# The filter's normalisation, one channel tile per attention step

## The chip, the cores and the metric

The kernel runs on one core of one Trainium2 chip. The metric is device time in microseconds of one execution, the median of several runs. Engines by their short names: PE (TensorE, matmuls; PEld its weight loads), DVE (VectorE), ACT (ScalarE), POOL (GpSimd), SP (which issues the DMAs).

## The reference, cut to what matters

One decoder block over 512 tokens of 1024 channels: an attention branch (16 heads, three kinds of keys) and a convolution branch, merged by sigmoid gates, then a projection, a SwiGLU feed-forward and a last norm. The change touches the middle of the convolution branch, a layer norm over the channels of each token and a Silu:

```
z  = u_a * sigmoid(u_b)                         # 512 tokens x 1024 channels
z  = causal_depthwise_conv(z, 31 taps) + conv_b
mu = mean(z, channels);  var = mean((z - mu)**2, channels)
zn = (z - mu) * rsqrt(var + EPS) * ln_g + ln_b
conv = silu(zn) @ w_conv_out + b_conv_out
```

## The kernel before

Activations lie with channels on the partitions: eight tiles `ct` of 128 channels x 512 tokens hold the filter's output. A sum over the channels is a matmul with `ones` (each entry 1/1024), which leaves the same mean in every partition.

The attention is a loop of 32 units (`n`): four key groups, two pairs of heads in each, four blocks of 128 queries. A unit first scores (`sc`: matmuls, maximum on DVE, exponential on ACT), then transposes the probabilities (`tP`), splits them into a high and a low part (`pth` by ACT, `ptl` by DVE) and multiplies with the values (`pv`). The loop interleaves the scoring of one unit with the second half of the last. Each step of it calls one piece of attention, then one of `taps`, then `fill`, which puts dense projections (`pch`, `ptk`) of some 520 ns of PE time between. All dense matmuls run as three products of high and low parts, whose weights ACT casts (`wh`) and POOL or DVE subtracts (`wl`).

`conv_taps` yields after every tap of a channel tile: one `scalar_tensor_tensor` on DVE, which accumulates in a PSUM bank (tag `cv`, one buffer; the loop's four tiles use it one after the other). In the loop run the taps of tiles 4 to 7, 4 x 31 steps.

`conv_norm` is called behind units 16, 17, 18, 20 and 21 (`stages`), each time with a whole stage: POOL sums the eight tiles (0); PE takes the mean over the partitions, ACT copies it to SBUF and DVE subtracts it from eight tiles (1); ACT squares and POOL sums (2); PE takes the variance, ACT the root by Sqrt and DVE its reciprocal (3); DVE multiplies eight tiles and ACT takes eight Silus, with the norm's scale and bias per channel (4). The sums over partitions use banks of tag `tr`, of which there are two and which the transposes use too; the squares use tiles of tag `pt`, five buffers, as `pth` and `ptl` do. At unit 24 `y_split` splits the eight tiles for the output projection.

The program is written in one order. Each engine's queue is then laid down before the run by a planner, which estimates when inputs are ready and buffers are free, and on the chip each engine runs its queue in that order.

Of the kernel before, what the change touches and what calls it, by code (L numbers as in the profile page):

```python
# [10 lines left out]
F32 = mybir.dt.float32  # L11
# [3 lines left out]
AF = mybir.ActivationFunctionType  # L15
OP = mybir.AluOpType
# [4 lines left out]
S = 512  # L21
KT = D // 128
NT = S // 128
# [5 lines left out]
EPS = 1e-6  # L29
# [7 lines left out]
def hybrid_block(  # L37
# [8 lines left out]
    nc = tc.nc  # L46
# [4 lines left out]
    cp = ctx.enter_context(tc.tile_pool(name="const", bufs=1))  # L51
# [5 lines left out]
    ps = psum_a.enter_context(tc.tile_pool(name="ps", bufs=1, space=PSUM))  # L57
# [4 lines left out]
    pa = astack.enter_context(tc.tile_pool(name="att", bufs=1))  # L62

    def acts(name, dt=F32):
        return ap.tile([128, S], dt, name=name, tag="A")

    def mid(name, tag="Z"):
        return bp.tile([128, 544 if tag == "Z" else S], F32, name=name, tag=tag)
# [10 lines left out]
    def scp(name):  # L79
        return ps.tile([128, 512], F32, name=name, tag="sc", bufs=2)  # L80

    def trp(name):
        return ps.tile([128, 512], F32, name=name, tag="tr", bufs=2)


    idn = cp.tile([128, 128], F32, name="idn")
# [3 lines left out]
    ones = cp.tile([128, 128], F32, name="ones")  # L90
    nc.vector.memset(ones, 1.0 / D)
    half = cp.tile([128, 4], F32, name="half")
    nc.vector.memset(half, -0.5)
    epsc = cp.tile([128, 1], F32, name="epsc")
# [67 lines left out]
    nc.tensor.transpose(pv0[:, :48], vst, idn[:48, :48])  # L162
    vec = cp.tile([128, 6, 8], F32, name="vec")
    nc.vector.tensor_copy(vec.rearrange("p a b -> p (a b)"), pv0[:, :48])
    g_mix, cb, lng, lnb, bco, g_ffn = (vec[:, i, :] for i in range(6))

    hT_hi = [acts(f"hThi{k}", F32R) for k in range(KT)]
    hT_lo = [acts(f"hTlo{k}", F32R) for k in range(KT)]
# [15 lines left out]
    for th in range(2):  # L184
# [6 lines left out]
        for k in range(KT):  # L191
            p = trp("hT")
# [161 lines left out]
    def ub_g(c, **kw):  # L354
        def ev(m, p):
            z = zs[2 * c + m]
            nc.vector.memset(z[:, 0:TAPS - 1], 0.0)
            z_done[0] = nc.scalar.activation(z[:, TAPS - 1:TAPS - 1 + S], p, AF.Tanh, scale=0.5).ins

        return chan_g(w_in, C_UB + 256 * c, hT_hi, hT_lo, ev, **kw)  # L360

    def ua_g(c):
        def ev(m, p):
            z = zs[2 * c + m][:, TAPS - 1:TAPS - 1 + S]
            nc.vector.scalar_tensor_tensor(z, z, 1.0, p, op0=OP.add, op1=OP.mult)

        return chan_g(w_in, C_UA + 256 * c, hT_hi, hT_lo, ev)

    def run_all(*gens):
        gens = list(gens)  # L370
        while gens:
            for g_ in list(gens):
                if next(g_, gens) is gens:
                    gens.remove(g_)
# [407 lines left out]
    def conv_taps(chans):  # L782

        acc = {}
        for k, c in enumerate(chans):
            cts[c] = mid(f"ct{c}", "C")
            acc[c] = ps.tile([128, 512], F32, name="cacc", tag="cv", bufs=1) if k == 0 else scp("cacc")
        for j in range(TAPS):
            for c in chans:
                z, a = zs[c], acc[c]  # L790
                if j == 0:
                    nc.scalar.activation(a, z[:, 0:S], AF.Identity, scale=cw[:, 0, c:c + 1], bias=cb[:, c:c + 1])  # L792
                else:
                    nc.vector.scalar_tensor_tensor(cts[c] if j == TAPS - 1 else a, z[:, j:j + S], cw[:, j, c:c + 1],  # L794
                                                   a, op0=OP.mult, op1=OP.add)
                yield 0

    norm = {}
    stages = [16, 17, 18, 20, 21]

    def conv_norm(stage):
        cc = [c[:, :S] for c in cts]
        if stage == 0:
            acc = pa.tile([128, S], F32, name="acc", tag="acc", bufs=1)
            nc.gpsimd.tensor_add(acc, cc[0], cc[1])
            for c in range(2, 8):
                nc.gpsimd.tensor_add(acc, acc, cc[c])
            norm["sum"] = acc
        elif stage == 1:
            p = trp("pstat")  # L810
            nc.tensor.matmul(p, ones, norm["sum"], start=True, stop=True)
            mean = pa.tile([128, S], F32, name="mean", tag="acc", bufs=1)
            nc.scalar.copy(mean, p)
            for c in range(8):
                nc.vector.tensor_sub(cc[c], cc[c], mean)
        elif stage == 2:
            acc = pa.tile([128, S], F32, name="acc2", tag="acc", bufs=1)
            nc.scalar.activation(acc, cc[0], AF.Square)
            for c in range(1, 8):
                sq = pa.tile([128, S], F32, name="sq", tag="pt", bufs=5)  # L820
                nc.scalar.activation(sq, cc[c], AF.Square)
                nc.gpsimd.tensor_add(acc, acc, sq)
            norm["sum"] = acc
        elif stage == 3:
            p = trp("pvar")
            nc.tensor.matmul(p, ones, norm["sum"], start=True, stop=True)
            rs = pa.tile([128, S], F32, name="rs", tag="acc", bufs=1)
            nc.scalar.activation(rs, p, AF.Sqrt, bias=epsc)
            nc.vector.reciprocal(rs, rs)
            norm["rs"] = rs  # L830
        elif stage == 4:
            for c in range(8):
                nc.vector.tensor_mul(cc[c], cc[c], norm["rs"])
            for c in range(8):
                nc.scalar.activation(cc[c], cc[c], AF.Silu, scale=lng[:, c:c + 1], bias=lnb[:, c:c + 1])

    ma, gcs = [], []
    phase["early"] = False
# [15 lines left out]
    def ga_g(g):  # L854
        gts[g] = [mid("gt") for _ in range(2)]
        return tanh_tiles(C_GA + 256 * g, [t_[:, :S] for t_ in gts[g]])
# [3 lines left out]
    def y_split():  # L860
        for c in range(8):
            cc = cts[c][:, :S]
            hi, lo = acts(f"yh{c}", F32R), acts(f"yl{c}", F32R)
            nc.scalar.copy(hi, cc)
            nc.vector.tensor_sub(lo, cc, hi.bitcast(F32))
            y_hi.append(hi)
            y_lo.append(lo)
# [53 lines left out]
    fin_v(*hid_v)  # L921
    qs[0, 1] = query_split(qds[0], 1)
    run_all(conv_taps((2, 3)))
    taps = itertools.chain(*(conv_taps((c,)) for c in range(4, 8)))
    work = []
    debt = [0.0]

# [10 lines left out]
    def fill_until(gen):  # L938
        while gen in work:
            c = next(work[0], None)  # L940
            if c is None:
                work.pop(0)
            elif c:
                debt[0] -= c
# [9 lines left out]
    for n in range(32):  # L954
        g, pr, i = n // 8, n // 4 % 2, n % 4
        if n % 8 == 0:
            for g_ in need:
                fill_until(g_)
            if g < 3:
                qds[g + 1] = []  # L960
                need = [query_dense(g + 1, qds[g + 1]), ga_g(g + 1)]
                work += ([ub_g(3), ua_g(3)] if g == 0 else []) + need
            if g == 0:
                gx = bp.tile([128, 1024], F32, name="gx", tag="gx", bufs=1)
                work.append(gc_g([gx[:, 0:512], gx[:, 512:1024]]))
            else:
                work.append(gc_key())
            if g:
                qs[g, 0] = query_split(qds[g], 0)
        if i == 0:  # L970
            ma.append(gts[g][pr])
        cur = unit(g, qs[g, pr], i, ma[-1], pr)
        na, nc_ = (2, 4, 4, 6)[i], ((n - 1) % 4 + 3 if n else 0)
        f = 520 if n < 24 else 800
        for gen in mixed(cur, na, pend, nc_):
            next(gen, None)
            next(taps, None)
            fill(f)
        pend = cur
        if n == 24:  # L980
            fill_until(work[-1] if work else None)
            y_split()
            work += [conv_out_g(c) for c in range(4)]
        if n == 25:
            qs[3, 1] = query_split(qds[3], 1)
            for t in range(2):
                load_x1(t, rp, "qd")
        elif g and n % 8 == 1:
            qs[g, 1] = query_split(qds[g], 1)
        if n == 29:  # L990
            while work:
                fill_until(work[-1])
            for ch in range(7):
                merge(ch)
        if n == 30:
            merge(7, (0,))
            phase["lo_dve"] = True
            work += [w_out_g(0, c) for c in range(2)]
        if n in stages:
            for _ in taps:  # L1000
                pass
            conv_norm(stages.index(n))
    for _ in pend:
        fill(800)
    while work:
# [116 lines left out]
    for t in range(NT):  # L1122
        sl = slice(128 * t, 128 * t + 128)

        for c in ((0, 256), (256, 512)) if t == NT - 1 else ((0, 512),):
# [5 lines left out]
            if j == 1 and t == NT - 1:  # L1131
                nc.vector.tensor_scalar(s01[:, t:t + 1], sums[:, t, 1:2], 1.0 / D, s01[:, t:t + 1], op0=OP.mult,
                                        op1=OP.add)
        r = cp.tile([128, 1], F32, name="rstd", tag="rstd", bufs=4)
# [6 lines left out]
                                       op0=OP.mult, op1=OP.mult)  # L1141
# [28 lines left out]
```

## Time and profile before

| | us |
|---|---|
| median of three runs (lowest, highest) | 975.17 (974.79, 975.36) |
| the profiled execution | 974.84 |
| its span, first to last instruction | 973.1 |
| PE busy | 940.4 |
| DVE, ACT, POOL busy | 633.1, 545.1, 234.9 |

The profile is of one execution. Times in it count from the first instruction. The attention loop runs from about 215 to 575 us. Busy time of PE is an upper bound of its work, since matmuls are pipelined and overlap.

### The profile page before, as it was taken

Reading aid. Unit: us, or ns where it says so; the run is one execution under the profiler, and the core shown is the slowest. Engines: PE = TensorE matmul, PEld = TensorE weight load, DVE = VectorE, ACT = ScalarE, POOL = GpSimd, SP = SyncE. Lnnn points to the kernel's source line nnn. Section 1 sums busy time; section 2 is a strip of 40 time slices with the busy share of each in tenths; the row PEclk is TensorE's granted clock in tenths of the full one; section 3 lists DMA queues with packets and bytes.
Section 4 is the critical chain, followed back from the end, with each engine's and each line's share of the span. In section 5 each row is a group of like instructions: output and inputs, shape, how many; then the busy total and the mean of one; then the engine's idle time right before and its main releaser. Section 6 shows DMA issues by size and latency. Waiting matters only on the chain.

```text
span 973.1 us, 14959 instructions
## 1 busy us (share of the span) xinstructions
PE 940.4 (97%) x5306; PEld 797.5 (82%) x5306; DVE 633.1 (65%) x1254; ACT 545.1 (56%) x1273; POOL 234.9 (24%) x256
## 2 busy tenths in 40 slices
PE   5999989899999999989999999999999999999996
PEld 5889979888888977877778878988888888888886
DVE  6799999987999987676876877633333343322512
ACT  6533545558879887999984776533333333322412
POOL 3545447853353342622322000000000000000000
PEclk9999989999999999999999999999999999999999
DMA  7333324542121111111212166633333323322302
GB/s 225 90 106 88 87 72 121 134 109 55 45 66 44 34 45 44 44 33 55 98 56 76 59 201 188 180 96 100 91 105 88 107 87 108 97 96 95 118 29 87
DMA packets 77599, 89.03 MB, mean 91 GB/s; under 512 B 5896, under 2 KB 65620, under 8 KB 77524
## 3 DMA queue, kind: packets, MB, share of 16 engines
q1 hardware_dynamic: 76676, 87.38, 30.0%
q8 instruction: 42, 0.69, 0.3%
q0 software_dynamic: 144, 0.52, 0.2%
q14 instruction: 33, 0.27, 0.1%
q10 hardware_dynamic: 704, 0.17, 0.1%
HBM read 85.96 MB, written 2.10 MB: 90 GB/s over the span
## 4 chain that ended last, share of the span: by engine, by line
PE 85%; DVE 7%; ACT 4%; issue 1%; DMA 1%; POOL 1%; SPq 0%; POOLq 0%; ACTq 0%; DVEq 0%
PE pf L211 8%; PE pf L212 8%; PE pf L213 8%; PE pch L213 7%; PE pch L211 7%; PE pch L212 7%; PE ptk L211 4%; PE ptk L212 4%; PE ptk L213 4%; PE pd L211 4%; PE pd L213 4%; PE pd L212 4%; PE tP L732 3%; PE sc L700 2%; PE sc L701 2%; PE pv L756 2%
## 5 line engine op out<-in xcount | busy, mean ns | idle before, releaser
L137 POOL TENSOR_TENSOR wl<-wr,wh 128x512 fp32r<-128x512 f32 x128 | 167.2, 1318 | 229.8 <-ACT wh L136 179.5
L136 ACT CAST wh<-wr 128x512 fp32r<-128x512 f32 x228 | 140.1, 622 | 145.0 <-PE pf L212 52.6
L794 DVE SCALAR_TENSOR_TENSOR cacc<-z,cw,cacc 128x512 f32<-128x512 f32 x232 | 165.5, 748 | 3.8 <-ACT cacc L792 1.7
L211 PE MATMUL pf<-h2hi,wh 128*128 128x512 f32 (+1 forms) x384 | 142.3, 372 | 0.6 <-ACT h2hi L1034 0.6
L212 PE MATMUL pf<-h2lo,wh 128*128 128x512 f32 (+1 forms) x384 | 142.5, 372 | 0.0
L213 PE MATMUL pf<-h2hi,wl 128*128 128x512 f32 (+1 forms) x384 | 142.4, 372 | 0.0
L137 DVE TENSOR_TENSOR wl<-wr,wh 128x512 fp32r<-128x512 f32 x100 | 68.7, 689 | 109.6 <-ACT wh L136 108.1
L213 PE MATMUL pch<-hThi,wl 128*128 128x512 f32 (+1 forms) x272 | 107.3, 395 | 1.5 <-POOL wl L137 1.5
L211 PE MATMUL pch<-hThi,wh 128*128 128x512 f32 (+1 forms) x272 | 107.3, 396 | 1.2 <-ACT hThi L195 1.2
L212 PE MATMUL pch<-hTlo,wh 128*128 128x512 f32 (+1 forms) x272 | 107.5, 396 | 0.0
L149 DVE TENSOR_TENSOR wl<-wr,wh 128x512 fp32r<-128x512 f32 x76 | 51.6, 689 | 61.9 <-ACT wh L148 61.8
L148 ACT CAST wh<-wr 128x512 fp32r<-128x512 f32 (+1 forms) x84 | 50.1, 604 | 73.7 <-PE pd L213 50.9
L708 ACT ACTIVATE P<-sc,nm 128x32 f32<-128x32 f32 (+3 forms) x192 | 84.7, 446 | 11.2 <-DVE nm L705 9.2
L1136 POOL TENSOR_TENSOR rstd<-rstd,half 128x1 f32<-128x1 f32 x4 | 2.2, 547 | 359.6 <-DVE rstd L1135 359.6
L211 PEld LDWEIGHTS pf<-h2hi,wh 128*128 128x128 f32 x384 | 72.0, 188 | 13.2 <-ACT h2hi L1034 0.8
L211 PE MATMUL ptk<-wh,hThi 128*128 128x256 f32 x288 | 82.7, 287 | 0.0
L213 PEld LDWEIGHTS pf<-h2hi,wl 128*128 128x128 f32 x384 | 72.2, 188 | 12.6
L212 PEld LDWEIGHTS pf<-h2lo,wh 128*128 128x128 f32 x384 | 72.2, 188 | 12.4
L212 PE MATMUL ptk<-wl,hThi 128*128 128x256 f32 x288 | 81.2, 282 | 0.0
L213 PE MATMUL ptk<-wh,hTlo 128*128 128x256 f32 x288 | 81.0, 281 | 0.0
L705 DVE TENSOR_REDUCE nm<-sc 128x1 f32<-128x32 f32 (+3 forms) x192 | 68.8, 381 | 16.8 <-PE sc L703 15.5
L211 PE MATMUL pd<-wh,ahi 128*128 128x512 f32 (+1 forms) x184 | 70.0, 380 | 0.8 <-DVE x L1092 0.8
(234 smaller groups left out, 2133.0 us busy)
## 6 DMA issues: line engine op xcount, KB each, us to landing
wr<-in_w_in_dram SPq DMA_DIRECT2D x100, 256.0 KB, 2.8
wr<-in_w_ffn_gate_dram SPq DMA_DIRECT2D x48, 256.0 KB, 2.7
wr<-in_w_ffn_up_dram SPq DMA_DIRECT2D x48, 256.0 KB, 2.7
wr<-in_w_ffn_down_dram SPq DMA_DIRECT2D x44, 256.0 KB, 2.5
wr<-in_w_out_dram SPq DMA_DIRECT2D x32, 256.0 KB, 2.6
x<-in_x_dram SPq DMA_DIRECT2D x8, 512.0 KB, 5.0
wr<-in_w_conv_out_dram SPq DMA_DIRECT2D x16, 256.0 KB, 2.7
wr<-in_cmp_k_w_dram SPq DMA_DIRECT2D x8, 256.0 KB, 2.6
```

The source lines that it names most:

```text
L136: nc.scalar.copy(hi[:, sl, :ncol], raw[:, sl, :ncol])
L137: eng.tensor_sub(lo[:, sl, :ncol], raw[:, sl, :ncol], hi[:, sl, :ncol].bitcast(F32))
L148: nc.scalar.copy(hi, raw)
L149: (nc.vector if phase["lo_dve"] else nc.gpsimd).tensor_sub(lo, raw, hi.bitcast(F32))
L211: nc.tensor.matmul(o, lh, rh, start=first, stop=False, skip_group_check=True)
L212: nc.tensor.matmul(o, lh, rl, start=False, stop=False, skip_group_check=True)
L213: nc.tensor.matmul(o, ll, rh, start=False, stop=last, skip_group_check=True)
L700: nc.tensor.matmul(sc[:, :e - a], qh[:, tsl], K[:, a:e], start=True, stop=False)
L705: nc.vector.tensor_reduce(out=nm[:, b:b + 1], in_=sc[:, ba - a:be - a], axis=AX.X, op=OP.max, negate=True)
L708: nc.scalar.activation(P[:, ba:be], sc[:, ba - a:be - a], AF.Exp, bias=nm[:, b:b + 1], accum_out=Dn[:, b, hh:hh + 1])
L732: nc.tensor.transpose(t4[:, 256 * b + 128 * hh:256 * b + 128 * hh + 128], Ps[hh][:, key_blk(j, b)], idn)
L794: nc.vector.scalar_tensor_tensor(cts[c] if j == TAPS - 1 else a, z[:, j:j + S], cw[:, j, c:c + 1], a, op0=OP.mult, op1=OP.add)
```

## The change

Stages are gone: `conv_norm` is now a generator, chained behind the taps, so that each step of the attention loop takes one piece of it. The mean stays in the bank `cv` and DVE subtracts from there; after each subtraction the same step squares on ACT and adds on POOL. The variance is taken by four matmuls with the sum of squares as weights and one column of `ones`, which puts it on 128 tokens by four columns; DVE adds EPS, POOL raises to the power -0.5, and four matmuls of the result, broadcast, with the identity spread it over the partitions into bank `cv` again. The Silu becomes x/2 (1 + tanh(x/2)): ACT writes the tanh to the bank `cv` and the halved affine to the tile, and DVE joins them by one `scalar_tensor_tensor`. `lnh` holds the halved scale and bias.

```
--- before.py
+++ after.py
@@ -162,7 +162,9 @@
     nc.tensor.transpose(pv0[:, :48], vst, idn[:48, :48])
     vec = cp.tile([128, 6, 8], F32, name="vec")
     nc.vector.tensor_copy(vec.rearrange("p a b -> p (a b)"), pv0[:, :48])
-    g_mix, cb, lng, lnb, bco, g_ffn = (vec[:, i, :] for i in range(6))
+    g_mix, cb, _, _, bco, g_ffn = (vec[:, i, :] for i in range(6))
+    lnh = cp.tile([128, 2, 8], F32, name="lnh")
+    nc.vector.tensor_scalar(lnh, vec[:, 2:4, :], 0.5, None, op0=OP.mult)
 
     hT_hi = [acts(f"hThi{k}", F32R) for k in range(KT)]
     hT_lo = [acts(f"hTlo{k}", F32R) for k in range(KT)]
@@ -795,44 +797,45 @@
                                                    a, op0=OP.mult, op1=OP.add)
                 yield 0
 
-    norm = {}
-    stages = [16, 17, 18, 20, 21]
-
-    def conv_norm(stage):
+    def conv_norm():
+
         cc = [c[:, :S] for c in cts]
-        if stage == 0:
-            acc = pa.tile([128, S], F32, name="acc", tag="acc", bufs=1)
-            nc.gpsimd.tensor_add(acc, cc[0], cc[1])
-            for c in range(2, 8):
-                nc.gpsimd.tensor_add(acc, acc, cc[c])
-            norm["sum"] = acc
-        elif stage == 1:
-            p = trp("pstat")
-            nc.tensor.matmul(p, ones, norm["sum"], start=True, stop=True)
-            mean = pa.tile([128, S], F32, name="mean", tag="acc", bufs=1)
-            nc.scalar.copy(mean, p)
-            for c in range(8):
-                nc.vector.tensor_sub(cc[c], cc[c], mean)
-        elif stage == 2:
-            acc = pa.tile([128, S], F32, name="acc2", tag="acc", bufs=1)
-            nc.scalar.activation(acc, cc[0], AF.Square)
-            for c in range(1, 8):
-                sq = pa.tile([128, S], F32, name="sq", tag="pt", bufs=5)
-                nc.scalar.activation(sq, cc[c], AF.Square)
+        acc = pa.tile([128, S], F32, name="acc", tag="acc", bufs=1)
+        for c in range(1, 8):
+            nc.gpsimd.tensor_add(acc, acc if c > 1 else cc[0], cc[c])
+            yield
+        mean = ps.tile([128, S], F32, name="pmean", tag="cv", bufs=1)
+        nc.tensor.matmul(mean, ones, acc, start=True, stop=True)
+        acc = pa.tile([128, S], F32, name="acc2", tag="acc", bufs=1)
+        for c in range(8):
+            nc.vector.tensor_sub(cc[c], cc[c], mean)
+            sq = acc if c == 0 else pa.tile([128, S], F32, name="sq", tag="pt", bufs=5)
+            nc.scalar.activation(sq, cc[c], AF.Square)
+            if c:
                 nc.gpsimd.tensor_add(acc, acc, sq)
-            norm["sum"] = acc
-        elif stage == 3:
-            p = trp("pvar")
-            nc.tensor.matmul(p, ones, norm["sum"], start=True, stop=True)
-            rs = pa.tile([128, S], F32, name="rs", tag="acc", bufs=1)
-            nc.scalar.activation(rs, p, AF.Sqrt, bias=epsc)
-            nc.vector.reciprocal(rs, rs)
-            norm["rs"] = rs
-        elif stage == 4:
-            for c in range(8):
-                nc.vector.tensor_mul(cc[c], cc[c], norm["rs"])
-            for c in range(8):
-                nc.scalar.activation(cc[c], cc[c], AF.Silu, scale=lng[:, c:c + 1], bias=lnb[:, c:c + 1])
+            yield
+
+        var = trp("pvar")
+        for t in range(NT):
+            nc.tensor.matmul(var[:, t:t + 1], acc[:, 128 * t:128 * t + 128], ones[:, 0:1], start=True, stop=True)
+        r = cp.tile([128, NT], F32, name="rvar")
+        nc.vector.tensor_scalar(r, var[:, :NT], EPS, None, op0=OP.add)
+        nc.gpsimd.tensor_tensor(r, r, half, op=OP.pow)
+        yield
+        rs = ps.tile([128, S], F32, name="prs", tag="cv", bufs=1)
+        for t in range(NT):
+            nc.tensor.matmul(rs[:, 128 * t:128 * t + 128], r[:, t:t + 1].to_broadcast([128, 128]), idn,
+                             start=True, stop=True)
+        for c in range(8):
+            nc.vector.tensor_mul(cc[c], cc[c], rs)
+            yield
+
+        for c in range(8):
+            th = ps.tile([128, S], F32, name="pth", tag="cv", bufs=1)
+            nc.scalar.activation(th, cc[c], AF.Tanh, scale=lnh[:, 0, c:c + 1], bias=lnh[:, 1, c:c + 1])
+            nc.scalar.activation(cc[c], cc[c], AF.Identity, scale=lnh[:, 0, c:c + 1], bias=lnh[:, 1, c:c + 1])
+            nc.vector.scalar_tensor_tensor(cc[c], th, 1.0, cc[c], op0=OP.add, op1=OP.mult)
+            yield
 
     ma, gcs = [], []
     phase["early"] = False
@@ -921,7 +924,7 @@
     fin_v(*hid_v)
     qs[0, 1] = query_split(qds[0], 1)
     run_all(conv_taps((2, 3)))
-    taps = itertools.chain(*(conv_taps((c,)) for c in range(4, 8)))
+    taps = itertools.chain(*(conv_taps((c,)) for c in range(4, 8)), conv_norm())
     work = []
     debt = [0.0]
 
@@ -979,6 +982,8 @@
         pend = cur
         if n == 24:
             fill_until(work[-1] if work else None)
+            for _ in taps:
+                pass
             y_split()
             work += [conv_out_g(c) for c in range(4)]
         if n == 25:
@@ -996,10 +1001,6 @@
             merge(7, (0,))
             phase["lo_dve"] = True
             work += [w_out_g(0, c) for c in range(2)]
-        if n in stages:
-            for _ in taps:
-                pass
-            conv_norm(stages.index(n))
     for _ in pend:
         fill(800)
     while work:
```

## Rows read from the trace of the kernel before

**Rows 1.** The page: busy time by engine; the chain that ended last.

```profile
PE 940.4 (97%) x5306; PEld 797.5 (82%) x5306; DVE 633.1 (65%) x1254; ACT 545.1 (56%) x1273; POOL 234.9 (24%) x256
...
PE 85%; DVE 7%; ACT 4%; issue 1%; DMA 1%; POOL 1%; SPq 0%; POOLq 0%; ACTq 0%; DVEq 0%
```

**Rows 2.** Stretches: width, busy PE, PEld, DVE, ACT, POOL (counts), PEclk, DMA share, GB/s.

```profile
300.00:310.00 10.00, 10.00 (x63) 8.06 (x62) 9.47 (x23) 9.77 (x28) 3.84 (x5) 1.00 0.20 55
360.00:370.00 10.00, 10.00 (x65) 8.37 (x63) 7.03 (x18) 8.57 (x23) 3.44 (x4) 1.00 0.15 38
380.00:390.00 10.00, 8.13 (x56) 6.55 (x54) 8.72 (x12) 7.68 (x20) 3.18 (x2) 1.00 0.12 28
390.00:400.00 10.00, 10.00 (x69) 9.19 (x70) 5.71 (x14) 8.66 (x22) 6.77 (x6) 0.83 0.08 26
410.00:420.00 10.00, 10.00 (x69) 8.56 (x68) 5.29 (x15) 9.86 (x34) 3.17 (x6) 1.00 0.10 27
430.00:440.00 10.00, 7.02 (x35) 5.41 (x34) 6.91 (x16) 9.98 (x20) 0.00 (x0) 0.96 0.08 26
440.00:450.00 10.00, 10.00 (x56) 8.15 (x56) 5.31 (x16) 8.37 (x24) 0.22 (x1) 0.87 0.01 2
460.00:470.00 10.00, 10.00 (x57) 8.32 (x56) 8.16 (x15) 9.95 (x29) 3.22 (x3) 1.00 0.06 19
```

**Rows 3.** Timeline, first hole: start us, us, engine, line, operation, [idle before].

```profile
379.87 1.02 PE L811 MATMUL pstat<-acc,ones 128*128 128x512 f32 x2
...
382.21 7.08 DVE L815 TENSOR_TENSOR ct<-ct,mean 128x512 f32<-128x512 f32 x8
...
389.94 0.38 PE L757 MATMUL pv<-ptl,v 128*128 128x256 f32 x1 [1.87 <-DVE ptl L736]
```

**Rows 4.** The timeline at the second hole.

```profile
430.50 5.05 ACT L835 ACTIVATE ct<-ct,vec 128x512 f32<-128x512 f32 x7
...
436.86 0.58 ACT L708 ACTIVATE P<-sc,nm 128x384 f32<-128x384 f32 x1
...
437.85 0.46 PE L700 MATMUL sc<-kst,qhi 128*128 128x416 f32 x1 [2.87 <-ACT P L708]
```

**Rows 5.** Views of lines 807, 811, 826: count, ns min/median/max, first and last start.

```profile
L807 POOL TENSOR_TENSOR acc<-acc,ct x6: 1280/1288/1310, 150.9 to 357.9; 128x512 f32<-128x512 f32 x6
...
L811 PEld LDWEIGHTS pstat<-acc,ones x2: 187/188/190, 379.6 to 379.9; 128*128 128x128 f32 x2
...
L826 PE MATMUL pvar<-acc,ones x2: 590/590/591, 417.7 to 418.2; 128*128 128x512 f32 x2
```

**Rows 6.** Views of single lines, columns as in rows 5.

```profile
L815 DVE TENSOR_TENSOR ct<-ct,mean x8: 681/683/1786, 382.2 to 387.5; 128x512 f32<-128x512 f32 x8
...
L833 DVE TENSOR_TENSOR ct<-ct,rs x8: 678/685/1717, 426.0 to 433.5; 128x512 f32<-128x512 f32 x8
...
L829 DVE RECIPROCAL rs<-rs x1: 3352/3352/3352, 421.5 to 421.5; 128x512 f32<-128x512 f32 x1
...
L835 ACT ACTIVATE ct<-ct,vec x8: 800/804/816, 428.2 to 434.8; 128x512 f32<-128x512 f32 x8
...
L821 ACT ACTIVATE sq<-ct x7: 614/618/627, 389.9 to 398.6; 128x512 f32<-128x512 f32 x7
...
L794 DVE SCALAR_TENSOR_TENSOR ct<-z,cw,cacc x8: 735/746/748, 85.9 to 355.5; 128x512 f32<-128x512 f32 x8
...
L792 ACT ACTIVATE cacc<-z,vec,cw x8: 772/782/786, 39.2 to 299.0; 128x512 f32<-128x512 f32 x8
...
L100 POOL TENSOR_TENSOR rstd<-rstd,half x8: 548/550/927, 6.2 to 605.8; 128x1 f32<-128x1 f32 x8
...
L732 PE MATMUL tP<-idn,P x320: 270/272/332, 215.5 to 567.4; 128*128 128x128 f32 x160
```

**Rows 7.** ACT's groups by line: the exponential's table loads; line 835's view.

```profile
L708 ACT ACT_TABLE_LOAD x3 | 3.8, 1283 | 2.2 <-DVE nm L705 2.1
...
L835 ACT ACT_TABLE_LOAD  x1: 1283/1283/1283, 426.9 to 426.9; - x1
```

## The prediction

> **What bounds the kernel now.** I read the page first. TensorE (PE) is busy in 940.4 of 973.1 us, and PE holds 85% of the chain that ended last, DVE 7%, ACT 4% [rows 1]. So a change of other engines' work counts only where PE waits for them or where its clock falls. The second view is the table by stretches: for most of the attention loop PE is busy 10.00 of 10 us at granted clock 1.00, and the exceptions near the normalisation are 380 to 390 (8.13), 390 to 400 (clock 0.83), 430 to 440 (7.02, clock 0.96) and 440 to 450 (clock 0.87) [rows 2]. Third, the timeline of the two holes, to see who ends them.
>
> First hole: DVE runs the eight subtractions of the mean in one block from 382.21 for 7.08 us. PE goes on with dense projections, then has no more, and waits 1.87 us, until 389.94, for `ptl`, which DVE makes only after the block [rows 3]. Second hole: ACT runs seven Silus as one block from 430.50 for 5.05 us and loads the exponential's table back, so that the exponential that frees a score bank starts at 436.86. PE's next score matmul, at 437.85, has waited 2.87 us for it [rows 4]. The clock falls behind each hole. A stretch of mean clock 0.83 holds 3.4 us at 1.2 GHz, which lose half, 1.7 us. For 0.96 and 0.87 it is 0.4 and 1.3 us. So the holes cost 1.87 + 1.7 = 3.6 and 2.87 + 1.7 = 4.6 us, 8.1 us together. That is what there is to gain.
>
> **The change, part by part.** The steps of the loop: the taps take 124; units 0 to 14 have 2, 7, 8, 11, 8, 7, 8, 11, ... steps, 119 together, so the taps end in the fifth of unit 15's eleven steps. The new generator has 32 steps: seven sums (units 15 and 16), eight of subtraction and square (16, 17), one for variance and root, eight multiplications (17, 18), eight of tanh (18, 19). A step lasts about 1.4 us: the mean's matmuls stand at 379.9 and the variance's at 417.7, 27 steps apart [rows 3, 5]. The queues are not in program order: sums written behind unit 16 ran from 150.9 on [rows 5], so an instruction goes forward once its inputs and buffers are there.
>
> Blocks that go. DVE: the subtractions stay 8 x 0.683 = 5.5 us (7.1 now, the longest took 1.786), multiplications 8 x 0.685 = 5.5, the reciprocal's 3.35 goes, and 8 `scalar_tensor_tensor` of 0.746 (the taps' row) = 6.0 come [rows 3, 6]. So 17.0 against 16.6 us, in single pieces, with attention's operations between them. That is the pattern of the taps (one 0.746 us operation a step), under which DVE stood at 9.47 and PE at 10.00 [rows 2, 6]. I cost this spreading at nothing. The work that hides it is PE's dense matmuls, which covered 5.2 of the 7.08 us even of the block [rows 3]. Without that cover it would cost one operation, 0.7 us, a step.
>
> ACT: now 8 x 0.62 squares, a copy of the mean and a root of the squares' size (estimated 0.62 each by their row), 8 x 0.804 Silu and four table loads of 1.283 (into root and Silu, and back to the exponential each time), 17.8 us together; after it 8 x 0.62 squares, 8 x 0.804 tanh and 8 x 0.782 Identity (the taps' first operation), 17.6 us [rows 6, 7]. Tanh already runs in this loop for the gates without loads of its own: the exponential's line has just three loads in the whole run [rows 7]. So the first hole's 3.6 us and the second's 4.6 go. What is late next is the tanh chain. Its one bank makes each channel wait for the last: 0.804 + 0.782 + 0.746 = 2.3 us, eight are 18.7 us, and ACT gets 12.7 us of them. ACT is 8.57 of 10 us busy here [rows 2], so 18.7 us have room for 2.7, and 10.0 us are over. Bounds: nothing, if dense work fills the delay as at 410 to 420 and 460 to 470, where ACT stands at 9.86 and 9.95 and PE at 10.00 [rows 2]; 10.0 us, if none does. The chain is interleaved with attention in pieces of 1.6 us, as those rows are and the 6.4 us block from 430.50 is not, so I take 1.0.
>
> PE: now two fp32 sums over 512 columns, two instructions each. A pair took 1.02 us to the end of the second, whose own length is 0.59, so 0.43 an instruction [rows 3, 5], 1.7 us in all. After it the mean keeps 0.86, the variance has four matmuls of one column and the root four of 128, each as two instructions: 16 small ones. I take the weight load's 0.188 us for each [rows 5], 3.0 us, so 2.1 us more. Bounds: 0.107 each (0.43 for 512 columns, cut to 128) is +0.9; the whole length of a 128-column transpose, 0.272 [rows 6], is +3.5.
>
> Waits added. The variance waits for the last subtraction, square and POOL addition, 0.683 + 0.618 + 1.288 = 2.6 us (the addition by the sums' row), and for one `wl` ahead on POOL, of the same size, estimated 1.3; the root waits for a four-column DVE operation (estimated 0.2, a full tile takes 0.68) and POOL's power of 0.55, behind a `wl` again: 2.0 [rows 5, 6]. Behind these matmuls stand PE's transposes and scores, and ACT's copies wait for those. Bounds 0 (they are moved back until ready, as now: the variance's sum, written at the end of unit 20, stands at 417.7 and no wait of PE is put to it) and 5.9 us. I take 0.5. The `sq` tiles also share five buffers with the `pt` tiles of the spreads; POOL needs 1.29 of each 1.4 us step for additions, so a copy may wait for it. The squares ran before in nearly that rhythm at 389.9 to 398.6 with PE at 10.00 [rows 2, 6], hence nothing, at most 1.3 us. The halving of the scales is one sixteen-column DVE operation at the start: an estimated 0.1, at most a full tile's 0.7.
>
> Sum, against the profiled execution's 974.84 us (span 973.1): -8.1 + 2.1 + 1.0 + 0.5 + 0.1 = -4.4, so 970.4. The median of the runs is 0.33 higher: 970.8.
>
> **The skill against the trace.** The stretched subtraction and multiplication (1.786 and 1.717 against 0.68) ran beside POOL's `wl`; taps with an operand in PSUM never passed 0.748 [rows 6]. The Trainium skill, "SBUF — State Buffer", section "SBUF: two separate sides", says that DVE with two SBUF inputs and GpSimd share a port pair as an exclusive lock. The trace agrees. By that rule, with mean and root in PSUM, this change drops the stretches: 2.1 us by the two longest rows, part of the block's gain above. Against the change speaks the Trainium skill's "Perfetto Trace Analysis", section "Optimizing Tensor Performance", which says that groups should rotate through several PSUM banks so that evacuation overlaps; here mean, root and eight tanh share one. By the rule the chain gets 18.7 us long, which is the third rival below.
>
> **The rivals.**
> 1. The saving is hidden anyway. At 460 to 470 ACT is at 9.95 [rows 2]; if ACT's total work bounds the loop, only ACT's 0.2 us is saved and PE waits later: 975.0. For it: ACT's share. Against: PE is at 10.00 in the same row.
> 2. PE waits in order at variance and root: 5.9 us in place of 0.5, so -8.1 + 2.1 + 1.0 + 0.1 + 5.9 = +1.0: 976.2. For it: one step separates producer and consumer in the program. Against: the queues move matmuls to where inputs are ready.
> 3. Slower: ACT is overloaded by the tanh chain at units 18 and 19. Its 10.0 us over, less the one cover of 3.5 us that the Silu block had (6.4 us of block, 2.87 of hole), is 6.5, and the clock falls again, 1.7. So -8.1 + 2.1 + 0.6 + 8.2 = +2.8: 978.0, and 981.5 without cover. It turns the sign from 5.4 us of waiting and clock together, and shows as slower from 7.4. For it: 12.7 us of ACT replace 6.4 of Silu and 2.6 of loads. Against: pieces of 1.6 us, and evacuations stand between them.
>
> **How the numbers follow.** The forecast has 0.60 and its own range is 967 to 973. Rival 1 has 0.16, rival 2 0.10, rival 3 0.14. What a measurement can tell from no change is 0.2%, 1.95 us: faster is below 973.2, slower above 977.1. Rivals 1 and 2 fall between, and some of the forecast's lower end too, against which some of rival 2 comes out at a gain: faster 0.61, same 0.24, slower 0.15. The range 966.5 to 978.0 leaves out the forecast's best tail and most of rival 3.
>
> **What would show it.** Right: no wait of PE over 1 us on `ptl` or on an exponential between 360 and 450, granted clock 1.00 there, no table load between the one before the first score and the one before the FFN's Silu, subtractions with a maximum near 0.75. Wrong: PE ended by DVE or POOL before `prs` or `pvar`; ACT at 10.0 of 10 in the tanh steps with PE under 9.5; new clock dips; the end of the loop not earlier although the holes are gone.

## The result: slower by 1.5%, against a forecast of faster

The changed kernel took 989.66 us (median, 989.31 to 989.93, 4 runs), the kernel before, on the same chip, 974.98 us (973.98 to 975.36, 4 runs). The ratio is 1.0152, 95% interval 1.0136 to 1.0168. Forecast were 970.8 us and a range of 966.5 to 978.0, so sign and range both failed.

The profile after, in the lines that answer to [rows 1]: page, busy time by engine, granted clock of TensorE in 40 slices, and the chain that ended last.

```profile
PE 950.3 (96%) x5320; PEld 802.8 (81%) x5320; DVE 628.3 (64%) x1263; ACT 546.0 (55%) x1275; POOL 234.7 (24%) x257
...
PEclk9999989999999999979999999999999999999999
...
PE 82%; ACT 6%; DVE 4%; POOL 3%; issue 3%; DMA 1%; SPq 0%; POOLq 0%; ACTq 0%; DVEq 0%
```

PE is still the bound (82% of the chain), but busy for 9.9 us more, ACT and POOL are more of the chain, and one slice has a clock of 0.7. The span of the profiled execution is 988.2 us, 15.1 more than before. To see where the time went I compare the two traces at equal work of PE: each matmul of both kernels counts as the usual distance of two starts of its shape (those of mean, variance and root don't count), and at each sum the clock of one trace is subtracted from that of the other. The lag of the kernel after grows and shrinks like this (times of the kernel before, us):

| stretch | lag grows by |
|---|---|
| 8 to 200, before the attention loop | +3.0 |
| 200 to 357, attention with taps | +0.4 |
| 357 to 374, mean and subtractions | +1.9 |
| 374 to 379, variance and root | +6.5 |
| 379 to 400, where the first hole was | -4.3 |
| 400 to 434, tanh steps | +14.4 |
| 434 to 445, where the second hole was | -5.4 |
| 445 to the end | -1.6 |
| sum | +15.1 |

Both holes are gone. Three things came that cost more. The stretches of the kernel after, columns as in [rows 2], in windows of 5 us:

```profile
380.00:385.00 5.00, 3.60 (x17) 2.22 (x15) 2.05 (x6) 4.53 (x16) 4.76 (x6) 1.00 0.01 3
385.00:390.00 5.00, 4.26 (x22) 3.62 (x22) 0.57 (x2) 1.40 (x3) 1.99 (x3) 0.70 0.00 0
...
400.00:405.00 5.00, 5.00 (x43) 4.55 (x42) 3.62 (x8) 5.00 (x15) 1.30 (x1) 1.00 0.14 28
405.00:410.00 5.00, 5.00 (x44) 4.73 (x43) 3.14 (x10) 4.95 (x9) 0.00 (x0) 1.00 0.09 30
410.00:415.00 5.00, 3.70 (x26) 2.99 (x25) 3.33 (x7) 5.00 (x13) 0.00 (x0) 1.00 0.00 0
415.00:420.00 5.00, 2.86 (x15) 1.58 (x13) 4.14 (x11) 4.95 (x14) 0.00 (x0) 1.00 0.00 0
420.00:425.00 5.00, 1.93 (x8) 1.25 (x9) 2.61 (x11) 5.00 (x9) 0.00 (x0) 0.61 0.00 0
425.00:430.00 5.00, 4.49 (x19) 3.70 (x18) 1.98 (x5) 3.56 (x16) 0.00 (x0) 0.50 0.00 0
430.00:435.00 5.00, 4.96 (x33) 4.16 (x32) 3.23 (x9) 4.12 (x14) 1.35 (x4) 0.86 0.01 3
```

From 400 to 425 ACT (the fourth busy number) is full almost without a break. For the first 10 us PE still runs at 5.00 beside it, on dense matmuls. Then these stop, and PE falls to 3.70, 2.86 and 1.93. The clock is at 1.2 GHz (0.50) from 421.1 to 431.3. From 410 to 435 PE is idle for 7.1 us, and it is busy in 7.0 of the 10.2 us of low clock, which costs 3.5: together 10.6 of the 14.4. The rest isn't parted here.

Why the dense matmuls stop stands in the timelines of PE and ACT (columns as in [rows 3]):

```profile
410.20 0.28 PE L215 MATMUL ptk<-wh,hTlo 128*128 128x256 f32 x1
...
420.56 0.58 ACT L618 ACTIVATE qd<-ptk 128x512 f32<-128x512 f32 x1
...
432.91 0.58 ACT L618 ACTIVATE qd<-ptk 128x512 f32<-128x512 f32 x1
...
434.72 0.48 PE L213 MATMUL pch<-hThi,wh 128*128 128x512 f32 x1
```

They had not run out. Dense sums use two PSUM banks (tag `dense`, two buffers), and ACT empties both by two copies each (`qd<-ptk`). The last matmul of the two sums starts at 410.20. ACT, full with attention and the tanh steps, comes to the first copy at 420.56 and to the second, which frees a bank, at 432.91. The next dense matmul (`pch`) stands at 434.72. So for 24.5 us PE has only attention's matmuls, and these wait for ACT too.

Attention in the same place:

```profile
421.03 0.71 ACT L725 ACTIVATE P<-P,R 128x512 f32<-128x512 f32 x1
...
421.65 0.77 ACT L835 ACTIVATE pth<-ct,lnh 128x512 f32<-128x512 f32 x1
...
421.80 0.69 PE L734 MATMUL tP<-idn,P 128*128 128x128 f32 x2 [1.13 <-ACT P L725]
...
422.97 0.80 ACT L836 ACTIVATE ct<-ct,lnh 128x512 f32<-128x512 f32 x1
...
424.43 1.54 PE L734 MATMUL tP<-idn,P 128*128 128x128 f32 x6 [1.94 <-ACT P L725]
```

Attention's own scaling of `P` (L725) alternates on ACT with the tanh (L835) and its affine (L836), and PE's transposes wait for the scaling, 1.13 and then 1.94 us. The other wait, at variance and root:

```profile
384.42 1.26 POOL L815 TENSOR_TENSOR acc<-acc,sq 128x512 f32<-128x512 f32 x1
...
385.74 1.05 PE L820 MATMUL pvar<-ones,acc 128*128 128x1 f32 x8 [2.09 <-POOL acc L815]
...
387.58 0.63 PE L744 MATMUL tPc<-idn,P 128*32 128x128 f32 x2
...
388.15 2.08 PE L827 MATMUL prs<-idn,rvar 128*128 128x128 f32 x8
```

PE waits 2.09 us for POOL's last sum of squares. It doesn't wait for the root, which POOL ends at 388.10: until then it has dense matmuls, a score and transposes (`tPc`). Behind the wait the clock falls to 1.2 GHz, from 387.0 to 390.4 (0.70 in that window), and the root's eight instructions run at it.

### The profile page after: what moved, and what is told of

The parts are those of the page before. It is cut to its first block, busy times and chain, and to the rows that moved or that the text cites. A ratio compares the mean times of both kernels' runs of the same rounds, so it can differ in the third digit from the quotient of the medians.

```text
span 988.2 us, 15004 instructions
## 1 busy us (share of the span) xinstructions
PE 950.3 (96%) x5320; PEld 802.8 (81%) x5320; DVE 628.3 (64%) x1263; ACT 546.0 (55%) x1275; POOL 234.7 (24%) x257
## 4 chain that ended last, share of the span: by engine, by line
PE 82%; ACT 6%; DVE 4%; POOL 3%; issue 3%; DMA 1%; SPq 0%; POOLq 0%; ACTq 0%; DVEq 0%
PE pf L213 8%; PE pf L214 8%; PE pf L215 8%; PE pch L214 7%; PE pch L215 7%; PE pch L213 7%; PE pd L213 4%; PE pd L215 4%; PE pd L214 4%; PE ptk L213 4%; PE ptk L214 4%; PE ptk L215 4%; PE tP L734 3%; PE sc L702 2%; PE sc L703 2%
## 5 line engine op out<-in xcount | busy, mean ns | idle before, releaser
L710 ACT ACTIVATE P<-sc,nm 128x32 f32<-128x32 f32 (+3 forms) x192 | 84.8, 447 | 10.2 <-DVE nm L707 8.2
L214 PEld LDWEIGHTS pf<-h2lo,wh 128*128 128x128 f32 x384 | 72.3, 188 | 12.3
```

What stands on the lines that cost most here:

```text
L214: nc.tensor.matmul(o, lh, rl, start=False, stop=False, skip_group_check=True)
L710: nc.scalar.activation(P[:, ba:be], sc[:, ba - a:be - a], AF.Exp, bias=nm[:, b:b + 1], accum_out=Dn[:, b, hh:hh + 1])
```

## The experiments

The runs before and after leave three suspects, namely the two new tiles, the tanh steps, and variance and root. The tanh steps have two explanations: ACT has too much to do at the tanh steps, or the one PSUM bank makes a chain of them.

**1. The kernel before, with two constant tiles more.** The growth before the attention loop has no changed instruction near it. What the change does there is to allocate two small tiles early, `lnh` and `rvar`, so that all later tiles lie 64 + 16 bytes per partition further on.

```diff
+    lnh = cp.tile([128, 2, 8], F32, name="lnh")
+    nc.vector.tensor_scalar(lnh, vec[:, 2:4, :], 0.5, None, op0=OP.mult)
+    rvar = cp.tile([128, NT], F32, name="rvar")
+    nc.vector.memset(rvar, 0.0)
```

> The kernel before, with the two small tiles of the change (lnh and rvar, 64 and 16 bytes a partition) allocated and written, and not used. In the changed kernel the 512-column matmuls of the first 200 us follow each other by 234 ns, before by 229, and 3.1 us are lost there, long before the normalisation. Theory A (the two tiles shift the addresses of the tiles that lie behind them, and PE reads its operands more slowly from there): the loss is here too, 3 us, 978, with 233 to 234 ns between the matmuls. Theory B (another order of the queues in the changed kernel, or chance): no loss, 975.0, 229 ns.

Measured: 977.58 us (975.48 to 979.49, 11 runs) against 974.88 (16 runs), ratio 1.0026 (1.0016 to 1.0035). Nobody reads the two tiles, and the kernel is slower by as much as the lag had grown. Stretches of the kernel before, the kernel after and this one, columns as in [rows 2]; the number in brackets behind PE's time counts matmuls:

```profile
100.00:120.00 20.00, 20.00 (x177) 19.79 (x176) 19.20 (x33) 10.85 (x25) 7.62 (x6) 1.00 0.32 92
```

```profile
100.00:120.00 20.00, 19.85 (x170) 19.47 (x169) 19.15 (x29) 10.68 (x25) 8.19 (x7) 1.00 0.32 83
```

```profile
100.00:120.00 20.00, 19.86 (x170) 19.48 (x169) 19.30 (x29) 10.57 (x24) 8.34 (x7) 1.00 0.31 81
```

At full clock and with PE all but full, fewer matmuls fit into the same 20 us, 170 in place of 177. The median distance between two starts of 128x512 is 234 ns in the kernel after (229 before), and 233 to 235 here.

**2. The kernel after, with the two tiles in old places.** The scales are halved where they lie, and the root uses the tag of the old `rstd` tiles.

```diff
-    lnh = cp.tile([128, 2, 8], F32, name="lnh")
-    nc.vector.tensor_scalar(lnh, vec[:, 2:4, :], 0.5, None, op0=OP.mult)
+    lnh = vec[:, 2:4, :]
+    nc.vector.tensor_scalar(lnh, lnh, 0.5, None, op0=OP.mult)
...
-        r = cp.tile([128, NT], F32, name="rvar")
+        r = cp.tile([128, NT], F32, name="rvar", tag="rstd", bufs=4)
```

> The changed kernel without the shift: the halved scales overwrite their place in vec, and the root takes a slot of the existing tag rstd. Theory A (addresses): 3.1 us faster than the changed kernel, 986.5, and 229 ns between the matmuls of the first 200 us. Theory B: 989.7.

Measured: 986.88 us (985.65 to 988.93, 4 runs), ratio 1.0120 (1.0106 to 1.0133), some 2.8 us less than the kernel after. The distance is 229 ns again, and the window from 100 to 120 has 173 matmuls. The lag up to 200 us falls to 1.8, not to 0. By the medians of 1 and 2 the placement is a cause of 2 to 3 us; what the other part of that lag is stays open. By which mechanism an address reaches the spacing of matmuls, no run here shows.

**3. The affine on POOL.** The first test of the tanh steps: `z/2` goes to POOL, and ACT keeps the bare tanh.

```diff
-            nc.scalar.activation(th, cc[c], AF.Tanh, scale=lnh[:, 0, c:c + 1], bias=lnh[:, 1, c:c + 1])
-            nc.scalar.activation(cc[c], cc[c], AF.Identity, scale=lnh[:, 0, c:c + 1], bias=lnh[:, 1, c:c + 1])
+            nc.gpsimd.tensor_scalar(cc[c], cc[c], lnh[:, 0, c:c + 1], lnh[:, 1, c:c + 1], op0=OP.mult, op1=OP.add)
+            nc.scalar.activation(th, cc[c], AF.Tanh)
```

> The changed kernel with the halved affine of the activation on POOL, ahead of the tanh, and the tanh without scale and bias, so that ACT gets one operation a tile in place of two (some 5 us in place of 12.6) while the bank cv and its chain stay, longer by POOL's 1.3 us a tile. Theory C (ACT has more than it can do in the tanh steps and PE waits for it, 13.9 us): 9 to 14 us faster than the changed kernel, 976 to 981, clock 1.00 at 420 to 435. Theory D (the single bank makes the chain of eight tiles the bound): no gain or slower, 989 to 994.

Measured: 979.08 us (977.33 to 979.36, 5 runs), ratio 1.0037 (1.0024 to 1.0050), 10.6 us less than after. The lag of the tanh steps is 1.5 instead of 14.4. The stretches:

```profile
410.00:420.00 10.00, 9.38 (x55) 7.28 (x54) 7.92 (x23) 9.90 (x26) 4.70 (x11) 1.00 0.00 0
420.00:430.00 10.00, 9.65 (x68) 7.99 (x66) 6.08 (x15) 9.29 (x33) 2.88 (x3) 1.00 0.30 80
```

PE is at 9.38 and 9.65 at full clock, where it had 6.56 and 6.42. ACT, though, is nearly as full as before. What differs in the trace is when it empties the two dense banks (view of line 618 from 395 to 440 us, columns as in [rows 5]):

```profile
L618 ACT ACTIVATE qd<-ptk x4: 570/574/611, 411.5 to 416.0; 128x512 f32<-128x512 f32 x4
```

With 7.8 us less on ACT the four copies stand at 411.5 to 416.0 in place of 420.6 to 436.3, and dense matmuls go on at 415.04; the first one waited 0.3 us for such a copy. The run leaves one thing undecided: without the affine behind it on ACT, each tanh also frees its bank sooner. Experiment 9 parts the two.

**4. One tanh tile every fifth step.**

```diff
             nc.vector.scalar_tensor_tensor(cc[c], th, 1.0, cc[c], op0=OP.add, op1=OP.mult)
-            yield
+            for _ in range(5):
+                yield
```

> The changed kernel with one tile of the activation in every fifth step in place of every step: the same operations, the same bank, spread over 40 steps in place of 8. Theory C (too much ACT work per step): 8 to 14 us faster than the changed kernel, 976 to 982. Theory E (what counts is that ACT got more work in total, wherever it lies, and the loop is bound by ACT): less than 4 us faster, 986 to 990.

Measured: 984.11 us (983.33 to 985.60, 4 runs), ratio 1.0091 (1.0077 to 1.0105), 5.5 us less than after. The result lies between the two expectations, and the lag of the tanh steps is 8.0. From 420 to 430 PE is at 7.44 of 10, and behind it the clock falls to 0.83 from 430 to 440.

Spreading the same work over 42 us in place of 23 takes 6.4 of the 14.4 us of lag away. ACT still is at 9.9 of 10 from 410 to 430, and no dense matmul starts from 419.9 to 433.2. So the pace counts, and so does the total; the run doesn't part them.

**5. Variance and root later.** Eight empty steps ahead of the variance, five more ahead of the root's matmuls; the tanh steps move by the same 13.

```diff
+        for _ in range(8):
+            yield
         var = trp("pvar")
...
         nc.gpsimd.tensor_tensor(r, r, half, op=OP.pow)
-        yield
+        for _ in range(6):
+            yield
```

> The changed kernel with eight empty steps between the last square and the variance's matmuls and five between the root and its matmuls; nothing else. Theory F (PE comes to these matmuls before POOL's last sum and power are done, waits in its queue's order and loses clock after it: some 6 us between 380 and 391): 4 to 7 us faster than the changed kernel, 983 to 986, no wait on pvar. Theory G (the cost is the sixteen small matmuls themselves and the squares on ACT and POOL): within 2 us of it, 988 to 991.

Measured: 979.51 us (978.79 to 980.30, 4 runs) against 975.34 (17 runs), ratio 1.0042 (1.0027 to 1.0057): 10.1 us less than after, more than was expected of the waits. The stretches:

```profile
380.00:385.00 5.00, 4.96 (x27) 3.62 (x26) 3.08 (x9) 4.78 (x18) 4.60 (x5) 1.00 0.08 27
385.00:390.00 5.00, 5.00 (x41) 4.43 (x40) 3.65 (x14) 4.94 (x14) 1.38 (x2) 1.00 0.00 0
...
425.00:430.00 5.00, 2.75 (x12) 2.11 (x12) 3.27 (x8) 4.95 (x15) 0.00 (x0) 0.51 0.00 0
```

PE has no wait for `pvar`, and full clock from 380 to 390. But the tanh steps were cheaper too, 8.0 of lag, so that this run alone doesn't say what the waits cost. Experiment 10 does.

**6. All three together** (2, 3 and 5).

> The changed kernel with the three changes together: no shift of the tiles, the affine on POOL, the root later. If the three causes are separate and add up (3 + 11 + 5 us): 989.7 - 19 = 970 to 972, faster than the kernel before. If the later root pushes the activation into steps where ACT is full again: 974 to 978.

Measured: 970.18 us (969.07 to 970.55, 5 runs) against 975.34, ratio 0.9947 (0.9934 to 0.9959). This is faster than both kernels. The stretches of the same place:

```profile
380.00:390.00 10.00, 10.00 (x80) 9.13 (x80) 6.97 (x21) 9.42 (x30) 2.74 (x4) 1.00 0.00 0
...
420.00:430.00 10.00, 8.93 (x49) 6.64 (x50) 7.69 (x21) 8.90 (x28) 5.72 (x8) 1.00 0.30 79
```

The granted clock is 1.00 from 380 to 440. The three single steps gave 2.8, 10.6 and 10.1 us, 23.5 together, and all of them 19.5: experiments 3 and 5 relieve in part the same tanh steps (experiment 10 has the share).

**7. The kernel before with only the tanh spread out.** Mean, variance and root stay in their blocks; tanh, affine and join replace the Silus, one tile a step behind unit 21.

```diff
-            for c in range(8):
-                nc.scalar.activation(cc[c], cc[c], AF.Silu, scale=lng[:, c:c + 1], bias=lnb[:, c:c + 1])
+    def tanh_steps():
+        for c in range(8):
+            ...
+            nc.scalar.activation(th, cc, AF.Tanh, scale=lnh[:, 0, c:c + 1], bias=lnh[:, 1, c:c + 1])
+            nc.scalar.activation(cc, cc, AF.Identity, scale=lnh[:, 0, c:c + 1], bias=lnh[:, 1, c:c + 1])
+            nc.vector.scalar_tensor_tensor(cc, th, 1.0, cc, op0=OP.add, op1=OP.mult)
+            yield
```

> The kernel before with the activation's part of the change alone: stages 0 to 3 and the eight multiplications as they were, then the tanh, Identity and join, one tile a step behind unit 21, in bank cv, without the shift. Theory C (the tanh and Identity are too much for ACT per step, whatever lies before them): the second hole (4.6 us) goes and some 14 us come, 982 to 986. Rival H (they cost so much only because the squares had left attention behind already): 971 to 976.

Measured: 977.72 us (977.24 to 978.83, 6 runs), ratio 1.0027 (1.0016 to 1.0038), between what was expected. The second hole's 5.4 us are gained, and 7.1 are lost behind it:

```profile
440.00:450.00 10.00, 8.67 (x43) 5.95 (x41) 5.14 (x14) 9.83 (x23) 0.43 (x1) 1.00 0.09 28
450.00:460.00 10.00, 8.44 (x44) 7.19 (x45) 6.48 (x15) 8.66 (x21) 0.00 (x0) 0.83 0.00 1
```

So the tanh in steps costs more than the hole that it removes, even with nothing else of the change.

**8. The same, with the affine on POOL** (the edit of 3 on 7).

> As the last, with the affine on POOL. Theory C: the second hole goes and little comes: 970 to 972, faster than the kernel before by 3 to 5 us. Rival I (POOL's eight operations delay the low parts of the weights, and PE waits for those): 974 to 978.

Measured: 974.51 us (972.92 to 975.65, 11 runs), ratio 0.9989 (0.9981 to 0.9998). The loss is gone, but a hole remains. From 430 to 440 POOL is full (10.00 of 10: six affines and two `wl` besides the rest of a third) and PE is at 7.19. What ends the wait is DVE:

```profile
432.15 5.20 DVE L835 TENSOR_TENSOR ct<-ct,rs 128x512 f32<-128x512 f32 x6
...
437.95 0.58 ACT L710 ACTIVATE P<-sc,nm 128x384 f32<-128x384 f32 x1 [4.03 <-DVE nm L707]
```

Six of the eight multiplications, which this kernel keeps in a block, hold up the maximum that ACT's exponential needs, and PE then waits 2.14 us for that exponential. So the time is within rival I's range, but the wait isn't the one that rival I names: no wait of PE is put to a `wl` there.

**9. The tanh into SBUF.** The affine stays on ACT, and the tanh goes into one of five buffers in place of the one PSUM bank.

```diff
-            th = ps.tile([128, S], F32, name="pth", tag="cv", bufs=1)
+            th = pa.tile([128, S], F32, name="th", tag="pt", bufs=5)
```

> The kernel after, but the tanh goes into one of the five `pt` tiles of SBUF in place of the single PSUM bank; its affine stays on ACT. Moving the affine to POOL in the third experiment also freed the bank sooner, so that run could not part ACT's load from the one bank. Theory C (ACT gets 1.58 us a tile for eight tiles where it is already busy): the 13.9 us at the tanh steps stay, within 3: 987 to 992, ACT 5.00 of 5 in 410 to 425, granted clock below 0.7 behind it. Theory D (each tanh waits for the join that frees the one bank, and attention queues behind that tanh): the lag of the tanh steps falls below 4, 977 to 981, as with the affine on POOL.

Measured: 986.98 us (986.16 to 988.84, 4 runs) against 975.52 (7 runs), ratio 1.0121 (1.0103 to 1.0139). That is 2.7 us less than after, 0.02 below the lower edge of the one theory and 6 above the other. The lag of the tanh steps is 11.0 in place of 14.4:

```profile
410.00:415.00 5.00, 1.16 (x10) 0.85 (x8) 2.42 (x7) 4.95 (x10) 0.00 (x0) 0.93 0.00 0
415.00:420.00 5.00, 3.96 (x12) 2.67 (x12) 2.75 (x5) 5.00 (x11) 0.00 (x0) 0.50 0.00 0
```

With the bank out of the way the tanh steps end sooner (last join at 420.4, not 423.8), and ACT, PE and clock show the same hole: the copies of the dense banks come at 422.3 to 426.0, and no dense matmul starts from 410.4 to 424.7. The bank of the tanh is worth about 3 us; the rest of the lag stays while ACT has the same work. No run moves the four copies ahead in ACT's queue, so it's open how much of the rest is the load and how much the order in which ACT took it.

**10. Only the tanh steps later**, by the 13 steps of experiment 5, with variance and root as in the kernel after.

```diff
+        for _ in range(13):
+            yield
         for c in range(8):
             th = ps.tile([128, S], F32, name="pth", tag="cv", bufs=1)
```

> The kernel after, but 13 empty steps stand between the multiplications and the tanh steps, so that these land in the steps where the fifth experiment had them; variance and root wait as in the kernel after. Theory F (the tanh steps cost by where they land: which attention and which dense work stand beside them): they cost 8.6 us as in the fifth experiment, not 13.9, and the waits keep their 6.5: 983 to 986. Theory G (they cost by how far attention is already behind because of variance and root): still 12 to 14: 988 to 991.

Measured: 986.48 us (986.41 to 987.08, 4 runs), ratio 1.0113 (1.0098 to 1.0128), between the two expectations. The lag of the tanh steps is 9.8, nearer to experiment 5's 8.0 than to the kernel after's 14.4: most of the difference is the place where they land. This run and experiment 5 differ in where variance, root and multiplications stand: 986.48 and 979.51, 7.0 us. So of experiment 5's 10.1, some 7.0 are put to these and 3.2 to the place of the tanh.

The lag by stretch (as in the table above) of the runs that rest on it, the lag at the end of the run, and, in the last column, the longest time at the tanh steps between the starts of two dense matmuls:

| kernel | to 200 | subtractions | variance, root | hole 1 | tanh | hole 2 | end of run | no dense matmul |
|---|---|---|---|---|---|---|---|---|
| after | +3.0 | +1.9 | +6.5 | -4.3 | +14.4 | -5.4 | 15.1 | 24.5 |
| 2, tiles unmoved | +1.8 | +1.9 | +6.7 | -4.1 | +15.2 | -5.4 | 14.1 | 25.2 |
| 3, affine on POOL | +2.1 | +1.9 | +6.6 | -3.8 | +1.5 | -5.3 | 2.5 | 4.9 |
| 5, root later | +3.7 | +1.9 | +0.5 | -2.1 | +8.0 | -5.1 | 5.5 | 12.0 |
| 9, tanh in SBUF | +3.2 | +1.9 | +6.4 | -4.0 | +11.0 | -5.5 | 11.9 | 14.3 |
| 10, tanh later | +2.8 | +1.9 | +7.4 | -3.3 | +9.8 | -5.3 | 12.3 | 15.8 |
| 6, all three | -0.5 | +1.9 | +0.5 | -1.3 | +1.0 | -5.2 | -5.8 | 2.9 |

These are of one profiled execution each; the medians above decide. The lag of the tanh steps goes roughly with the last column. The first column holds another difference too: near 140 us the clock is at 1.2 GHz for 6.8 us in the kernels before and after and in 2, 5 and 9, for 3.4 us in 3, 6 and 10.

## Why the prediction was wrong

The step that failed is the price of the tanh chain: "The chain is interleaved with attention in pieces of 1.6 us, as those rows are and the 6.4 us block from 430.50 is not, so I take 1.0." It cost 14.4 us, or 15.4 with the variance's old matmuls (1.02 us by [rows 3]) that left the stretch. The step itself worked out that ACT would be 10.0 us over. Then it set that aside because of two windows in which ACT stood at 9.86 and 9.95 and PE at 10.00 [rows 2]. It took the dense matmuls for a cover that doesn't depend on ACT. But ACT empties their two banks, and once it was late with that, the cover was gone: after 10 us beside a full ACT no dense matmul started for 24.5 us. The rival stood in the text as the third, with a chance of 0.14 and 978.0 to 981.5 us. It had the right place, an overloaded ACT, and its size was too small: 8.2 to 11.7 us with 1.7 of them for the clock, against 15.4 with some 3.5. Experiment 3 removes 7.8 us of ACT's work and 10.6 us of time; 9 leaves the work and removes the tanh's bank, and 2.7 us go.

The idea of a cover that is used up is in the reading of the first hole too ("then has no more"), and the trace before speaks against it: the dense sum `ptk` that stops at 387.79 goes on at 391.08. The rest of it stood behind the waiting `pv` in PE's queue.

Point by point, against the terms of the sum:

- Holes, -8.1. Right, 8.7 us. The second brought -5.4, the first -3.3 (-4.3 less the 1.02 us of the mean's matmuls, which moved to 363.6). No table load is left between 380 and 440, and the subtractions are no longer stretched (view of line 811, columns as in [rows 5]):

```profile
L811 DVE TENSOR_TENSOR ct<-ct,pmean x8: 645/670/681, 365.0 to 378.9; 128x512 f32<-128x512 f32 x8
```

- Small matmuls, +2.1. The number is right in part by luck: 1.02 for the mean, 1.05 and 2.08 for variance and root, less 2 x 1.02 that went, are 2.1, but the 2.08 are at 1.2 GHz. In experiment 6, at full clock, the root's matmuls take 1.27 us, which makes the sum 1.3, within the bounds.
- Waits at variance and root, 0.5 within 0 to 5.9. Wrong: 3.4 us at the spot (6.5 less 3.1 of matmuls), of which 2.09 are the wait for the variance's sum and none a wait for the root. By experiments 10 and 5 it is 7.0, past the upper bound, which includes what it does to the stretches behind it. "They are moved back until ready, as now" didn't hold: the queue had `pvar` ahead of POOL's last sum, with two gate products of attention (L772, L773) in between on POOL. That was rival 2, at 0.10, right for the variance and not for the root.
- Spreading on DVE, 0. Nearly right: some 0.9 us remain of the 1.9 once the mean's 1.02 is taken off, and the two waits of PE in that stretch, 0.25 and 0.74 us, are that size. No run here separates them. (DVE's 16.6 us before are 16.5 by the three blocks in the trace, 7.08, 6.09 and 3.35; nothing hangs on it.)
- Halving of the scales, +0.1, at most 0.7. Wrong in kind: the tile of the halved scales and the root's tile shift all others, and that is 2 to 3 us by experiments 1 and 2. No rival held this.

With the placement, the waits and the affine set right (experiment 6), the kernel takes 970.18 us. That it is 0.6 under the forecast is chance, for it is another kernel, without the tanh's second operation on ACT. But the gain of the two holes was there, and the change as written spent it nearly three times over elsewhere (some 9 us of gain against 24 of losses).

On the two pages that the prediction weighed. The Trainium skill, "SBUF — State Buffer", section "SBUF: two separate sides", says that DVE with two SBUF inputs and GpSimd reading SBUF lock each other out. The trace agrees: with the mean in PSUM no subtraction passed 0.681 us, though two ran beside POOL's `wl` (from 372.30) and one beside its sum of squares (from 373.56). In experiment 8, where the root is in SBUF, multiplications took up to 1.77 us and POOL's affines up to 2.25, side by side.

The Trainium skill, "Perfetto Trace Analysis", section "Optimizing Tensor Performance", has independent matmul groups rotate through different PSUM banks, so that ACT's or DVE's evacuation overlaps the next group. That speaks of matmul groups; the tanh's bank is written by ACT, and taking it away (experiment 9) brought 2.7 us, where taking the second operation from ACT (experiment 3) brought 10.6. The dense groups do rotate through two banks, and it didn't help them while ACT was late: both stood full until the second copy, at 432.91, had emptied one.

## What to carry to other kernels

A window in which an engine is full and PE is full too doesn't show that more work on that engine is covered. Before adding work to an engine at 86%, ask what the covering matmuls need from it: here ACT empties the two banks of the dense sums, so that its delay stopped the cover itself. Price what lies beyond at the idle time plus the low clock that follows. Work moved to an idle engine (the affine on POOL) recovered more than spreading it over time on the busy one. And an added tile, however small, can shift all the addresses behind it, so try the change once with the tiles where they were.

## What the runs showed that I had not expected

- Two constant tiles of 64 and 16 bytes per partition moved the median distance of two 128x512 matmuls from 229 to 234 ns, and of 128x256 from 113 or 114 to 117, for the first 190 us; in the attention loop 128x512 went from 232 to 235, and the FFN at the end kept its 227 ns.
- POOL's power over 128x4 took 1.03 us; over 128x1 it has a median of 0.55 [rows 6].
- POOL's affine of a 128x512 tile takes 0.77 to 0.80 us in experiment 6 (up to 2.25 in experiment 8), its additions of two such tiles 1.26 to 1.29 us in the kernel after.
